# A list scheduler learns three more facts about the engines: the VectorE and GpSimd lock, measured durations, and the rate of a broadcast DMA

## The chip, the cores and the metric

The kernel runs on one core of one Trainium2 chip. The metric is the device time of one execution in microseconds (us), lower is better. A core has five instruction queues that run in order, each for itself: TensorE (PE, matmuls; its weight loads are listed as PEld), VectorE (DVE), ScalarE (ACT), GpSimd (POOL), and SyncE (SP), which issues the DMAs. Semaphores hold an instruction back until what it needs is there.

## The reference

The program is one block of a generator with two layers over 256 latent tokens and a prefix of 256 context tokens, 1024 features each, in float32. Cut to its frame:

```python
for layer in range(DEPTH):                       # DEPTH = 2
    mod_l, mod_c = ...                           # shift, scale, gate from silu(c) @ ada_w[layer]
    h = modulate(rmsnorm(x, g), shift, scale)    # latent and context tokens
    x = x + gate * (rglru_mixer(h) if layer == 0 else deltanet_mixer(h))
    h = modulate(rmsnorm(x, g2), shift2, scale2)
    x = x + gate2 * swiglu(h, w_gu, w_down)      # 1024 -> 2 x 2816 -> 1024
return rmsnorm(x, final_norm_g)                  # latent tokens
```

Layer 0 mixes tokens with a bidirectional gated linear recurrence (RG-LRU: input product, short convolution, gates, scan in both directions, output product). Layer 1 mixes them with a bidirectional gated DeltaNet: input product, short convolution and SiLU on q, k and v, then for each head and each chunk of tokens a unit triangular system is solved, and a state is carried over the chunks in both directions. Each layer ends in a SwiGLU feed-forward part.

## The kernel before

**Work.** Features lie on the 128 partitions, tokens along the free dimension. Every float32 product is made of three faster ones: a weight tile is loaded as `raw` [128, 1024], split into a high part `whi` and a remainder `wlo` (`weight()`, lines 636 to 646), and activations are split in the same way (`hh`, `hl`). `mm3()` issues whi with hh, whi with hl, wlo with hh into one PSUM bank. The copy that makes whi may go to ACT or DVE. The subtraction that makes wlo may go to DVE or POOL in layer 0, in both feed-forward parts and in the late DeltaNet work, and is fixed to POOL in most of the DeltaNet layer. There are three `raw` buffers and two each of `whi` and `wlo`.

**Stages.** 0 to about 240 us: modulation and the RG-LRU layer. 240 to 690: its output, the feed-forward part of layer 0, and the background sums of layer 1's modulation (`ada_steps`, tiles `x` and `ring`). 690 to 1275: the DeltaNet layer. 1275 to the end: the feed-forward part of layer 1. In the DeltaNet layer the program text runs stages in the order of the string `PROG`: A (input products; `conv_silu` evicts each product from PSUM by four operations that write `cu`, then SiLU), E (decays: a DMA spreads one row of the small DRAM array `rows` over all partitions into `gn`, eight affine_selects on POOL mask it, ACT takes exponentials), N (the triangular systems: `gn` is scaled, four 32-row transposes on DVE bring the diagonal blocks into `lw`, thirty pairs of `lmul` and `lw` operations on DVE solve them, two more transposes write `ld` and `ldt`), L (the off-diagonal blocks by small matmuls into `ps_w` and `ps_z`), P (attention weights: the same spread of `rows` into `qg`, affine_selects into `at`), C (the state: `ps_ks`, `ps_y`, `ps_s`, `ps_o`, with `kw`, `vb`, `S`, `oa`; a power on POOL gives `fo`, the norm of an output head; `nkh` is the like for a key head), Z and W (output gates and the output product). `scratch` holds the small tiles of the decay computation at the stage's start.

**Order.** Nothing is issued as written. Every instruction becomes an `_Op` of the `Recorder`, with its operands, its dependencies, a priority (its place in the text plus a bias per stage from `TUNE`), and for each engine that may run it a cost from `_cost()` (lines 257 to 296). At the end of a part of the program `flush()` (line 364 on) runs a list scheduler: it keeps a clock for each of the five engines, always takes the engine whose clock is least (PE, then DVE, ACT, POOL, SP at a tie), and gives it the ready instruction with the lowest priority number. `bank_free()` (line 475) says when the PSUM bank of an instruction is free of other engines; an instruction that would start over 40 ns later than its engine's clock is put back until then, and the engine takes another. An instruction with a choice is left to the other engine if that one would be done sooner. DMAs share one modelled channel of 360 bytes per ns with 2000 ns latency. Tiles take their buffers in program order. The order found is then emitted engine by engine, and the hardware queues run it strictly in that order, whatever the real durations are. So a cost does not change what an instruction takes; it changes the order of the queues and which engine gets an instruction.

Of the kernel before, what the change touches and what calls it, by code (L numbers as in the profile page):

```python
# [12 lines left out]
F32 = mybir.dt.float32  # L13
# [13 lines left out]
# columns of the packed small-parameter array  # L27
# [10 lines left out]
# ---------------------------------------------------------------- program order  # L38
# The kernel is written down stage by stage; a list scheduler then orders the instructions of all
# engines, earlier stages first, so that later independent work fills an engine's waits. Tiles are  # L40
# allocated when their first instruction is placed.
def _shuffle(sh, pattern, sizes):
    """einops-like rearrange of a numpy array"""
# [33 lines left out]
class _Tile:  # L77
    def __init__(self, pool, shape, dtype, tag, bufs, name, dram):
# [7 lines left out]
        # a bank of PSUM is one region: its readers wait for all products into it  # L86
# [6 lines left out]
        self.group = [-1] * 4       # last product into the bank, per 32 partitions  # L93
        self.used = {}              # a bank serves one engine at a time: its last use by each
# [5 lines left out]
class _AP:  # L100
    """an access pattern of a tile that may not have its place yet"""
# [34 lines left out]
    def raw(self, offset, ap):  # L136
        """any pattern over a DRAM tile"""
        return self._with(("raw", offset, ap), self.sh)
# [25 lines left out]
class _Op:  # L164
    __slots__ = ("alts", "args", "kw", "tiles", "deps", "prio", "idx", "bytes", "succ", "ndep", "ready", "fin", "rows", "cols", "narrow")


_TABLE = {"Tanh": 7, "Exp": 1, "Gelu_apprx_tanh": 2, "Silu": 4, "Sqrt": 8}     # sets that hold the function
# [28 lines left out]
class Recorder:  # L197
    DMA_RATE = 360.0        # bytes / ns
    DMA_LATENCY = 2000
    TICK, TICK_COLUMNS = 10240 / 3, 3300  # L200
    # from the end of an instruction to the start of one that waits for it
# [15 lines left out]
    # ---- instructions with a choice of engine  # L217
# [22 lines left out]
    def tt(self, out, a, b, op):  # L240
        """add, subtract or mult of SBUF operands"""
        self._any(("DVE", "tensor_tensor", (out, a, b, op), {}), ("POOL", "tensor_tensor", (out, a, b, op), {}))

    @staticmethod
    def mark(ap):
        """the instructions that have written ap so far, for after= of a later one"""
        return np.unique(ap.t.writer[ap.blocks()]).tolist()
# [8 lines left out]
    # ---- costs in ns  # L256
    def _cost(self, eng, method, out, ins, kw, args):
        n = out.free() if isinstance(out, _AP) else 1
        src_psum = any(i.t.psum for i in ins) or (isinstance(out, _AP) and out.t.psum)
        if eng == "PE":  # L260
# [8 lines left out]
            if m <= 64:         # the column groups run side by side  # L269
                first = out.sh.flat[0] < out.t.sh.size // 4  # L270
                return (max(4 * w / 2.4, 54) + 2) if first else 27 if m <= 32 else 54
            return max(4 * w / 2.4, 213) + 4
        if eng == "DVE":
            if method == "transpose":
                return 1.04 * n + 70
# [12 lines left out]
        if eng == "POOL":  # L288
            if method == "dma_start":
                return 1000  # L290
            if method in ("memset", "affine_select"):
                return 0.6 * n + 60
            if kw.get("op", args[3] if len(args) > 3 else None) == OP.pow:
                return 165 * n + 298
            return 2.2 * n + 100
        return 60

# [3 lines left out]
    def add_any(self, alts):  # L301
        """one instruction, on whichever of its engines is free first; alts hold the same operands"""
# [11 lines left out]
        op.alts = {}  # L314
        for eng, m, fn, a2, k2 in alts:
# [4 lines left out]
            op.alts[eng] = (self._cost(eng, m, out, ins, k2, a2), table, fn, a2, k2)  # L320
        op.bytes = 0
        if method == "dma_start":
            x = outs[0] if outs and not outs[0].t.dram else ins[0]
            op.bytes = 128 * 4 * x.free()
        eng = alts[0][0]
        op.rows = min(ins[0].sh.shape[0], 4) / 4 if eng == "PE" else 0      # share of the array's rows
        op.narrow = eng == "PE" and ins[0].free() <= 32
        op.cols = 0         # columns through the whole array
# [26 lines left out]
        if eng == "PE":     # accumulation groups of a bank stay in order  # L355
# [7 lines left out]
    # ---- order and emit  # L363
    def flush(self):
# [10 lines left out]
        # slots: the tiles of a tag take them in program order  # L375
# [27 lines left out]
        def offer(op):  # L403
            """all dependencies placed: a candidate once its tiles have slots"""
# [23 lines left out]
        dma_free, table, done = 0.0, 1, 0  # L428
        at_tick, columns, slow, rows, narrow = 0, 0.0, False, 1, False
        order = []  # L430
        while done < len(ops):
# [26 lines left out]
            if e == "PE" and op.rows != rows:  # L458
                # another tiling of the array costs a refill: stay with this one for a while
# [15 lines left out]
            def bank_free(op, e):  # L475
                return max((f + self.LATENCY[x][e] for t in op.tiles if t.psum for x, f in t.used.items() if x != e),
                           default=0.0)

            wait = bank_free(op, e)
            if len(op.alts) > 1:  # L480
                # leave it to another engine that would be done sooner
# [7 lines left out]
            if e == "PE":  # L489
                # the array runs at half its clock in a tick after one that kept it idle  # L490
# [23 lines left out]
            fin = clock[e]  # L514
            if op.bytes:
# [37 lines left out]
def hybrid_block(ctx: ExitStack, tc: tile.TileContext, I, out, dbg=None):  # L553
# [18 lines left out]
    def bank(tag, name="ps"):  # L572
        if tag == "mm" and cur["wide"]:     # the products take all banks but one in turn
# [11 lines left out]
    # ---------------------------------------------------------------- loads and constants  # L585
# [28 lines left out]
    # silu(c), silu(c_ctx) as the stationary operand of the modulation products  # L614
# [4 lines left out]
    sel4 = cp.tile([128, 2], F32, name="sel4")      # sums over the column groups of both streams  # L619
# [8 lines left out]
    # ---------------------------------------------------------------- weight streaming  # L628
# [7 lines left out]
    def weight(*src, cols=1024, aside=False, place=None):  # L636
        """hi + lo parts of a weight tile; aside: not on DVE"""
# [12 lines left out]
    def ahead(*srcs):  # L650
        """weights of the first products after this stage"""
# [11 lines left out]
    # ---------------------------------------------------------------- adaLN modulation  # L663
# [1056 lines left out]
```

## Time and profile before

| | |
|---|---|
| median of 3 runs | 1481.32 us (1480.1 to 1487.81) |
| span of the profiled execution | 1474.6 us; the page gives no time for what lies around it |
| instructions | 23548 |
| mean granted TensorE clock | 0.934 |
| ACT busy | 552.4 us (37%) |
| bytes moved by DMA | 208.26 MB, mean 141 GB/s |

How to read the lines of the profile: a row of the timeline gives start and length in us, engine, source line, operation, `out<-in` by tile names, shape, count, and in brackets how long the engine was idle before it and what ended that. All instructions carry line 544, where the order is emitted; they are told apart by tile names. A row of the waits gives the waiting engine and tile, what it waited for, total us, times and the longest. A row of the groups gives count, busy us, mean ns of one, and the idle time before the group. A row of the DMA list gives count, size and the median us from issue to landing.

### The profile page before, as it was taken

The page shows a single profiled execution, that of the slowest core. Times are in us where ns is not written, and L with a number is a line of the kernel's source. Part 1 is how long each engine was busy: PE and PEld are TensorE (multiplying, and loading weights), DVE is VectorE, ACT ScalarE, POOL GpSimd, SP SyncE. Part 2 cuts the span into 40 slices and gives each one's busy share as a digit, 9 for nine tenths or more (in the row PEclk, how much of TensorE's full clock was granted, in tenths as well). Part 3 has the DMA queues.
Part 4 walks back from the last instruction along what each step waited for, and adds up shares of the span by engine and source line. Part 5 has one row for each costly group of instructions (what it writes and reads, how often), then busy time and mean ns, then how long its engine had stood idle before and what let it go on. Part 6 is the DMA issues. An engine that isn't in the chain of part 4 may idle for free.

```text
span 1474.6 us, 23548 instructions
## 1 busy us (share of the span) xinstructions
PE 1329.7 (90%) x9195; PEld 1135.7 (77%) x9195; DVE 1149.3 (78%) x1802; ACT 552.4 (37%) x1069; POOL 430.8 (29%) x357
## 2 busy tenths in 40 slices
PE   6998989999999999988767997888888898899997
PEld 3676758787778777886656786777788797899997
DVE  6899996778888885577689578699698767777765
ACT  3365562342323231025666434735634531211100
POOL 2134341111122111122545332643543521122111
PEclk9999999999999999999978789699599899999999
DMA  9544433355544564333842115315235205455563
GB/s 355 193 146 142 155 115 104 139 190 190 177 171 172 173 206 120 105 123 122 190 132 90 50 56 131 95 65 151 88 100 136 95 12 181 139 186 180 177 186 116
DMA packets 69790, 208.26 MB, mean 141 GB/s; under 512 B 6960, under 2 KB 14384, under 8 KB 69424
## 3 DMA queue, kind: packets, MB, share of 16 engines
q1 hardware_dynamic: 69680, 206.77, 44.1%
q8 instruction: 72, 1.18, 0.3%
q14 instruction: 38, 0.31, 0.1%
HBM read 196.71 MB, written 10.03 MB: 140 GB/s over the span
## 4 chain that ended last, share of the span: by engine, by line
PE 28%; DVE 17%; issue 3%; DMA 3%; POOL 1%; ACT 1%; POOLq 0%; SPq 0%; DVEq 0%; ACTq 0%
PE ps_mm L544 13%; DVE lw L544 4%; PE ps_dn L544 4%; DVE cu L544 3%; DVE lmul L544 2%; DMA qg<-rows 2%; PE ps_z L544 2%; PE ps_wo L544 2%; PE ps_w L544 2%; PE ps_y L544 2%; DVE whi L544 1%; PE ps_o L544 1%; DVE gn L544 1%; PE ps_g L544 1%; PE ps_s L544 1%
## 5 line engine op out<-in xcount | busy, mean ns | idle before, releaser
L544 PE MATMUL ps_mm<-hh,whi 128*128 128x512 f32 (+1 forms) x888 | 340.6, 385 | 35.3 <-DVE cu L544 18.2
L544 PE MATMUL ps_mm<-hh,wlo 128*128 128x512 f32 (+1 forms) x888 | 337.6, 381 | 18.1 <-POOL wlo L544 12.3
L544 PE MATMUL ps_mm<-hl,whi 128*128 128x512 f32 (+1 forms) x888 | 337.4, 381 | 0.3 <-DVE hl L544 0.3
L544 POOL TENSOR_TENSOR wlo<-raw,whi 128x1024 fp32r<-128x1024 f32 (+1 forms) x69 | 171.9, 2493 | 379.4 <-DVE whi L544 141.9
L544 DVE CAST whi<-raw 128x1024 fp32r<-128x1024 f32 (+1 forms) x185 | 139.3, 753 | 136.9 <-PE ps_mm L544 68.2
L544 PEld LDWEIGHTS ps_mm<-hh,whi 128*128 128x128 f32 x888 | 178.6, 202 | 73.6 <-issue 26.7
L544 DVE TENSOR_TENSOR wlo<-raw,whi 128x1024 fp32r<-128x1024 f32 (+1 forms) x169 | 214.7, 1271 | 11.3 <-ACT whi L544 1.4
L544 PEld LDWEIGHTS ps_mm<-hh,wlo 128*128 128x128 f32 x888 | 178.6, 201 | 50.0 <-POOL wlo L544 14.9
L544 PEld LDWEIGHTS ps_mm<-hl,whi 128*128 128x128 f32 x888 | 178.7, 201 | 29.0 <-issue 1.6
L544 PE MATMUL ps_dn<-fh,wlo 128*128 128x256 f32 (+1 forms) x374 | 122.5, 328 | 0.9 <-DVE wlo L544 0.9
L544 PE MATMUL ps_dn<-fh,whi 128*128 128x256 f32 (+1 forms) x374 | 122.9, 329 | 0.3 <-DVE whi L544 0.3
L544 PE MATMUL ps_dn<-fl,whi 128*128 128x256 f32 (+1 forms) x374 | 122.3, 327 | 0.0
L544 PE MATMUL ps_mm<-h2h,whi 128*128 128x256 f32 x352 | 100.1, 285 | 1.2 <-ACT h2h L544 1.2
L544 PE MATMUL ps_mm<-h2l,whi 128*128 128x256 f32 x352 | 100.5, 286 | 0.2
L544 PE MATMUL ps_mm<-h2h,wlo 128*128 128x256 f32 x352 | 100.1, 285 | 0.1
L544 POOL TENSOR_TENSOR x<-x,ring 128x1024 f32<-128x1024 f32 x13 | 37.0, 2850 | 166.3 <-ACT ring L544 166.3
L544 ACT ACTIVATE whi<-raw 128x1024 fp32r<-128x1024 f32 (+2 forms) x53 | 54.7, 1033 | 79.6 <-PE ps_mm L544 32.9
L544 ACT ACTIVATE fh<-sg 128x256 fp32r<-128x256 f32 (+1 forms) x43 | 22.4, 522 | 157.7 <-DVE sg L544 157.7
L544 PEld LDWEIGHTS ps_dn<-fh,wlo 128*128 128x128 f32 x374 | 71.1, 190 | 7.7 <-DVE wlo L544 1.8
L544 PEld LDWEIGHTS ps_dn<-fh,whi 128*128 128x128 f32 x374 | 71.1, 190 | 7.5 <-DVE whi L544 0.7
L544 ACT ACTIVATE ring<-ring,cs 128x1024 f32<-128x1024 f32 x42 | 48.3, 1150 | 74.3 <-DVE x L544 74.2
L544 PEld LDWEIGHTS ps_dn<-fl,whi 128*128 128x128 f32 x374 | 71.1, 190 | 5.9
(309 smaller groups left out, 2868.0 us busy)
## 6 DMA issues: line engine op xcount, KB each, us to landing
ring<-ada_w SPq DMA_DIRECT2D x96, 512.0 KB, 4.7
raw<-ffn_gu SPq DMA_DIRECT2D x88, 512.0 KB, 3.6
raw<-dn_w_in SPq DMA_DIRECT2D x49, 512.0 KB, 3.5
raw<-ffn_down SPq DMA_DIRECT2D x34, 512.0 KB, 3.6
raw<-rg_w_in SPq DMA_DIRECT2D x16, 512.0 KB, 3.8
gn<-rows SPq DMA_DIRECT2D x4, 2048.0 KB, 15.5
raw<-ffn_down SPq DMA_DIRECT2D x17, 384.0 KB, 3.4
raw<-dn_w_out SPq DMA_DIRECT2D x12, 512.0 KB, 3.5
```

The source lines that it names most:

```text
L544: call(*[real(x) for x in args], **{n: real(v) for n, v in kw.items()})
```

## The change

Only the model inside the scheduler changes; stage order, biases, buffers and arithmetic stay as they are.

1. *Durations.* The DVE transpose costs 1.85 ns per column in place of 1.04; on POOL affine_select and memset get prices of their own, and other operations go from 2.2 n + 100 to 2.25 n + 30 ns.
2. *Lock.* Each instruction gets a class per engine from `_lock()`. On DVE class 1 is an operation with two wide SBUF inputs, class 2 a `tensor_copy` or `tensor_scalar` from SBUF to SBUF, 0 the rest, such as all that read only one tensor from SBUF beside PSUM. On POOL memset is class 2, all else but DMAs class 1. `flush()` keeps in `held` the end and class of the last operation of the other engine, and `bank_free()` also waits for that end where both classes are set and either DVE's is 2 or POOL's is 1.
3. *Broadcast.* A DMA from a pattern made by `.raw()` (the loads of `gn` and `qg` from `rows`) counts 2.3 times its bytes.

```diff
         if eng == "DVE":
             if method == "transpose":
-                return 1.04 * n + 70
+                return 1.85 * n + 70
...
-            if method in ("memset", "affine_select"):
-                return 0.6 * n + 60
+            if method == "affine_select":
+                return 1.1 * n + 30
+            if method == "memset":
+                return 0.87 * n + 25
             if kw.get("op", args[3] if len(args) > 3 else None) == OP.pow:
                 return 165 * n + 298
-            return 2.2 * n + 100
+            return 2.25 * n + 30
         return 60
+
+    @staticmethod
+    def _lock(eng, method, outs, ins):
+        if eng == "DVE":
+            wide = [x for x in ins if not x.t.psum and x.free() > 1]
+            if len(wide) > 1 or (len(wide) == 1 and method == "tensor_tensor" and len([x for x in ins if not x.t.psum]) > 1):
+                return 1
+            if method in ("tensor_copy", "tensor_scalar") and len(wide) == 1 and not outs[0].t.psum:
+                return 2
+            if method == "tensor_tensor" and len(ins) == 1 and wide:
+                return 1
+            return 0
+        if eng == "POOL":
+            return 2 if method == "memset" else 1 if method != "dma_start" else 0
+        return 0
...
+            op.lock[eng] = self._lock(eng, m, outs, ins)
...
             op.bytes = 128 * 4 * x.free()
+            if any(o[0] == "raw" for y in ins for o in y.ops):
+                op.bytes *= 2.3
...
             def bank_free(op, e):
-                return max((f + self.LATENCY[x][e] for t in op.tiles if t.psum for x, f in t.used.items() if x != e),
+                free = max((f + self.LATENCY[x][e] for t in op.tiles if t.psum for x, f in t.used.items() if x != e),
                            default=0.0)
+                mine, (until, theirs) = op.lock[e], held.get(e, (0.0, 0))
+                if mine and theirs:
+                    dve, pool = (mine, theirs) if e == "DVE" else (theirs, mine)
+                    if dve == 2 or pool == 1:
+                        free = max(free, until)
+                return free
...
             clock[e] += cost
             fin = clock[e]
+            if e in ("DVE", "POOL"):
+                held["POOL" if e == "DVE" else "DVE"] = (clock[e], op.lock[e])
```

More of the change, by code (lines that the diff above doesn't have):

```diff
@@ L164 @@
 class _Op:
-    __slots__ = ("alts", "args", "kw", "tiles", "deps", "prio", "idx", "bytes", "succ", "ndep", "ready", "fin", "rows", "cols", "narrow")
+    __slots__ = ("alts", "args", "kw", "tiles", "deps", "prio", "idx", "bytes", "succ", "ndep", "ready", "fin", "rows", "cols", "narrow",
+                 "lock")
 _TABLE = {"Tanh": 7, "Exp": 1, "Gelu_apprx_tanh": 2, "Silu": 4, "Sqrt": 8}
@@ L313, in add_any @@
         op.args, op.kw = a, k
-        op.alts = {}
+        op.alts, op.lock = {}, {}
         for eng, m, fn, a2, k2 in alts:
@@ L427, in flush @@
                 offer(op)
-        dma_free, table, done = 0.0, 1, 0
+        dma_free, table, done, held = 0.0, 1, 0, {}
         at_tick, columns, slow, rows, narrow = 0, 0.0, False, 1, False
```

## The prediction

> **What bounds the kernel now.** I read the head of the page first, then the busy times of the first three of four stages, then the list of who TensorE (PE) waits for, and last the instructions around the longest of its waits.
>
> ```profile
> span 1474.6 us, 23548 instructions
> PE 1329.7 (90%) x9195; PEld 1135.7 (77%) x9195; DVE 1149.3 (78%) x1802; ACT 552.4 (37%) x1069; POOL 430.8 (29%) x357
> 0.00:240.00 240.00, 215.43 (x1075) 152.13 (x1076) 205.01 (x316) 121.34 (x181) 68.27 (x58) 0.98 0.51 179
> 240.00:690.00 450.00, 435.75 (x2225) 356.29 (x2223) 347.26 (x415) 133.89 (x195) 84.32 (x41) 0.99 0.46 156
> 690.00:1275.00 585.00, 488.51 (x4326) 438.23 (x4325) 460.49 (x897) 275.70 (x640) 244.54 (x230) 0.85 0.37 106
> ```
>
> The columns of a stage are its length, then busy time of PE, weight loads, VectorE (DVE), ScalarE (ACT) and GpSimd (POOL), then the granted clock. In the first feed-forward stage (row two) PE is idle for 14.3 of 450 us: no order of the other engines can win much there, nor in the second one, which is built in the same way. The RG-LRU stage (row one) leaves 24.6 us idle, and the DeltaNet stage (row three) 96.5 us at a mean clock of 0.85. What the change can win lies there, in the waits of PE. The first six rows are of the DeltaNet stage, the last two of the RG-LRU stage:
>
> ```profile
> PE ps_mm L544 <- DVE cu L544: 18.2, 7, 6.2
> PE ps_mm L544 <- ACT whi L544: 8.7, 1, 8.7
> PE ps_mm L544 <- POOL wlo L544: 7.2, 4, 4.8
> PE ps_ot L544 <- DVE lmul L544: 4.6, 1, 4.6
> PE ps_mm L544 <- DVE lw L544: 4.6, 1, 4.6
> PE ps_mm L544 <- POOL wlo L544: 5.1, 3, 2.7
> PE ps_mm L544 <- POOL ol L544: 1.8, 1, 1.8
> ```
>
> **Part 1, the lock.** The planner now knows that DVE and POOL hold each other up. Is that so? At 798.8 us:
>
> ```profile
> 798.86 2.48 DVE L544 TENSOR_TENSOR lmul<-lw 128x168 f32<-128x168 f32 x1
> 801.27 0.73 DVE L544 SCALAR_TENSOR_TENSOR cu<-ps_mm,sm,cu 128x508 f32<-128x508 f32 x1
> 801.92 1.81 DVE L544 TENSOR_TENSOR lw<-lw,lmul 128x168 f32<-128x168 f32 x1
> 798.80 4.75 POOL L544 TENSOR_TENSOR wlo<-raw,whi 128x1024 fp32r<-128x1024 f32 x2 [2.79 <-DVE whi L544]
> 1015.41 0.32 DVE L544 TENSOR_TENSOR lmul<-lw 128x168 f32<-128x168 f32 x1
> 1015.76 0.33 DVE L544 TENSOR_TENSOR lw<-lw,lmul 128x168 f32<-128x168 f32 x1
> 1015.50 1.10 POOL L544 TENSOR_TENSOR nkh<-ssk,phalf 128x4 f32<-128x4 f32 x1 [7.41 <-DVE nbc L544]
> 687.08 0.29 DVE L544 SCALAR_TENSOR_TENSOR scratch<-scratch 128x128 f32<-128x128 f32 x1
> 688.54 2.75 DVE L544 SCALAR_TENSOR_TENSOR scratch<-scratch 128x128 f32<-128x128 f32 x2
> 691.87 2.00 DVE L544 SCALAR_TENSOR_TENSOR scratch<-scratch 128x128 f32<-128x128 f32 x1
> ```
>
> It is: lmul took 2.48 us and lw 1.81 beside two POOL wlo, and 0.32 and 0.33 elsewhere, while cu, which reads PSUM, kept its 0.73. Behind the two stood cu, the evictions that free the bank for PE: the longest of the seven cu waits. The lock cost (2.48 - 0.32) + (1.81 - 0.33) = 3.6 us of it. The scratch operations before another such wait lost (2.75 - 2 x 0.29) + (2.00 - 0.29) = 3.9 us. In the new plan DVE finds lmul blocked and takes cu first, which it classes as free. I take both: -7.5; bounds 0 (cu was not ready) and -18.2 (all seven). Late next at 799 is wlo itself, which ends at 803.55.
>
> In the RG-LRU stage PE waits 5.1 + 1.8 = 6.9 us for POOL. With the lock counted, an operation that may go to either engine looks dearer on POOL:
>
> ```profile
> L544 POOL TENSOR_TENSOR wlo<-raw,whi 128x1024 fp32r<-128x1024 f32 x13 | 36.8, 2832 | 67.6 <-ACT whi L544 24.8 <-PE ps_g L544 15.0 <-DVE whi L544 12.2
> L544 DVE TENSOR_TENSOR wlo<-raw,whi 128x1024 fp32r<-128x1024 f32 x15 | 18.3, 1222 | 0.8
> L544 DVE SCALAR_TENSOR_TENSOR iu<-iu,u 128x512 f32<-128x512 f32 x16 | 19.7, 1233 | 0.0
> 122.80 0.68 DVE L544 SCALAR_TENSOR_TENSOR iu<-iu,u 128x512 f32<-128x512 f32 x1
> ```
>
> Moving a wlo costs DVE 1.22 us and spares it a lock of up to 2.83; DVE is busy for 205 of 240 us, so it can't take all. Half of the wait: -3.5; bounds -6.9, and +7.1 if all thirteen move (13 x 1.22 = 15.9 us more on DVE) and only what iu lost to the lock (19.7 - 16 x 0.68 = 8.8 us) is won back.
>
> **Part 2, the broadcast's rate.** A DMA from the `rows` array now counts 2.3 times its bytes: 2.10 MB at 360 bytes/ns is 5.8 us plus 2, and becomes 13.4 plus 2.
>
> ```profile
> gn<-rows SPq DMA_DIRECT2D x4, 2048.0 KB, 15.5
> 717.14 0.69 DVE L544 CAST whi<-raw 128x1024 fp32r<-128x1024 f32 x1 [0.20 <-PE ps_mm L544]
> 719.22 5.67 POOL L544 TENSOR_SCALAR_AFFINE_SELECT gn<-gn 128x512 f32<-128x512 f32 x8 [4.44 <-DMA gn<-rows]
> 724.87 2.34 POOL L544 TENSOR_TENSOR wlo<-raw,whi 128x1024 fp32r<-128x1024 f32 x1
> 727.27 0.79 PE L544 MATMUL ps_mm<-hh,wlo 128*128 128x512 f32 x1 [4.82 <-POOL wlo L544]
> 1129.64 0.64 POOL L544 TENSOR_SCALAR_AFFINE_SELECT at<-qg 128x512 f32<-128x512 f32 x1 [10.10 <-DMA qg<-rows]
> 1130.25 1.01 POOL L544 TENSOR_TENSOR fo<-sso,nhalf 128x4 f32<-128x4 f32 x1
> 1132.55 1.09 PE L544 MATMUL ps_ot<-ident,oa 128*128 128x128 f32 x4 [4.62 <-DVE lmul L544]
> ```
>
> The chip took 15.5 us, so the new figure fits. The old one made POOL's queue wait: it stood idle 4.44 us for gn with a wlo behind the eight selects whose cast had ended at 717.83, and PE then waited 4.82 us for that wlo. At 1129.64 POOL had stood 10.10 us for qg with fo behind it, and PE waited 4.62 us for the transposes that need it. A planner that expects the broadcast later puts wlo and fo first: -9.4; bounds 0, and -11.8 if the rest of that stage's 7.2 us for POOL wlo goes with it. SP's queue gains nothing: the broadcasts keep their places, and a weight load behind one still lands late (PE's 8.7 us for ACT whi stays).
>
> **Part 3, the durations.** The affine_select and memset prices change little that anyone waits for; the transpose is the one that counts.
>
> ```profile
> L544 DVE STREAM_TRANSPOSE lw<-gn 32x1024 f32<-32x1024 f32 x16 | 31.6, 1978 | 0.2
> 728.29 0.63 PE L544 MATMUL ps_mm<-hl,whi 128*128 128x512 f32 x1
> 728.71 0.63 PE L544 MATMUL ps_mm<-hh,wlo 128*128 128x512 f32 x1
> 731.23 0.40 PE L544 MATMUL ps_mm<-hh,whi 128*128 128x512 f32 x1
> 731.47 0.39 PE L544 MATMUL ps_mm<-hl,whi 128*128 128x512 f32 x1
> ```
>
> It was planned at 1.04 x 1024 + 70 = 1135 ns, takes 1978, and is now planned at 1964. The DVE time is the same; only what stands between the transposes can move. In the 4.6 us wait on lw, cu stood behind three transposes, each 0.84 us longer than planned: -2.5; bounds 0 and -4.6. With the waits goes some slow clock: after the gap of 4.82 us PE's matmuls started 0.42 us apart instead of 0.24, and by 731.2 they were back. If the slow pace held from 727.3 to 731, those are nine matmuls x 0.18 us: 1.6 us. Four such gaps close in parts 1 and 2, 6.4 us; half, since the rows show it after one gap only: -3; bounds 0 and -6.4.
>
> **What it adds.** The choice of engine, the release of slots and all later orders follow the new clock, with the stage order and the biases unchanged. Two costs show in no row. The rule lets POOL start only when DVE's last locking operation is over, and at a tie DVE is taken first, so behind a run of such operations POOL is planned late; above, the chip let a wlo in between two of them. And a power on four columns counts as a lock for about 1 us, while nkh (1.10 us) ran beside lmul and lw of 0.32 and 0.33.
>
> By the Trainium skill (SBUF — State Buffer, "Who interferes with whom") a DVE instruction with two SBUF inputs contends with any GpSimd instruction that reads SBUF, and the first to issue blocks the other for the whole instruction. By that rule the charge for the powers is right, and the half of the next cost that I lay to it would go: 1466.5 in place of 1469. The nkh row speaks against it.
>
> ```profile
> L544 POOL TENSOR_TENSOR wlo<-raw,whi 128x1024 fp32r<-128x1024 f32 (+1 forms) x40 | 95.5, 2390 | 105.5 <-ACT whi L544 50.2 <-DVE whi L544 16.4 <-DVE lw L544 15.0
> ```
>
> PE's products need these forty, and behind each stand POOL's kw, vb and S and the next weight load, whose buffer it frees. If one wlo in each of the four lmul/lw runs comes a whole wlo late, that is 4 x 2.39 = 9.6 us; if none, 0: I take +4.8. Below 0 it can't lie: what DVE gains from a later POOL is in part 1. A new head of a queue somewhere is priced by the longest of PE's waits above, 8.7 us; with none, 0. I take one: +8.7.
>
> **The sum.** -7.5 - 3.5 - 9.4 - 2.5 - 3 + 4.8 + 8.7 = -12.4 us on the span of 1474.6. The median of the runs, 1481.32, stands 6.7 us above that span, which I keep: 1468.9, so 1469.
>
> **The rivals.** *Slower: POOL is planned late as a rule.* Place: the forty wlo of the DeltaNet stage. For it speaks that DVE is busy 460 of 585 us there, much of it in locking operations; against it, that POOL is busy only 245 and the chip grants it the lock in its turn. If every second one is a wlo late on PE's path, 20 x 2.39 = 48 us are lost against gains of 26: +22, 1503. It decides from about eleven late wlo on; a handful more than that gives 1489.
>
> *No change.* The planned waits close, but DVE bounds the stage (460 of 585 us): it is busy through the whole gap at 799, so PE's gaps move behind the next eviction. Then parts 1 and 3 give nothing, part 2 its 9.4, the costs stay at some 9 to 13: 1481 to 1485, at 1481.
>
> *All gains, no costs*: -26, 1455; POOL's 71% of free time speaks for it, the fixed biases against.
>
> **How the numbers follow.** Forecast 0.42, all gains 0.10, no change 0.21, slower 0.27. What a measurement can tell from no change is about 0.5%, 7.4 us; the forecast and the full gain lie beyond it: faster 0.52, same 0.21, slower 0.27. The range runs from 1448 (below the full gain, with part 1 nearer its bound) to 1497 (half of the slower cases); the likeliest case alone spans 1460 to 1474.
>
> **What would show it.** Part 1: DVE's wlo-side stretches shrink (lmul, iu and scratch nearer 0.3 to 0.7 us), and PE's wait for cu falls from 18.2 to about 10. Part 2: POOL's idle before gn and at falls, with wlo or fo ahead of them in its queue. Part 3: the wait on lw goes. Wrong it is if PE's wait for POOL wlo in the DeltaNet stage rises past 20 us, or if the stage's idle time stays at 96 us with other names in the list.

## The result: 1481 to 1430 us, and the profile after

The changed kernel takes 1429.7 us, the median of four runs (1424.51 to 1431.86), beside 1480.71 us for the kernel before in the same runs: a ratio of 0.965 with an interval of 0.9605 to 0.9694. The direction was forecast, the size was not: -51 us in place of -12.4. The profiled execution took 1428.36 us and has a span of 1426.6. Ratios, here and below, leave out executions more than 1.5% above the fastest of their kernel; among the kernels below this takes out two of wait_pool's four, and the profiled one of both_l0, which took 2109.43 us at a granted clock of 0.558.

Head of the page after:

```profile
span 1426.6 us, 23481 instructions
PE 1308.5 (92%) x9195; PEld 1126.8 (79%) x9195; DVE 1092.5 (77%) x1843; ACT 590.2 (41%) x1119; POOL 293.0 (21%) x273
```

PE has the same 9195 matmuls and is idle 118.1 us instead of 144.9; it is also busy 21.2 us less for the same work. GpSimd lost 84 of its 357 instructions and a third of its busy time, and VectorE, which took 41 more, is busy 57 us *less*.

To compare stages, both traces are cut, to within 0.6 us, at the same five places: the first output product of the RG-LRU layer, the first down product, the first key transposes of the DeltaNet layer, the first product of the last feed-forward part, and the end. First before, then after; columns as in the prediction, with DMA share and rate last.

```profile
0.00:208.80 208.80, 187.19 (x958) 130.38 (x959) 183.97 (x287) 113.08 (x167) 66.09 (x57) 0.98 0.54 190
208.80:525.90 317.10, 306.31 (x1507) 245.28 (x1505) 255.69 (x282) 99.06 (x135) 54.99 (x22) 1.00 0.47 162
525.90:680.70 154.80, 148.37 (x780) 124.68 (x781) 103.68 (x144) 35.77 (x57) 26.86 (x17) 0.98 0.41 130
680.70:1269.70 589.00, 493.21 (x4358) 442.13 (x4356) 464.14 (x901) 279.38 (x650) 249.19 (x232) 0.86 0.38 108
1269.70:1474.60 204.90, 194.64 (x1596) 193.24 (x1596) 141.84 (x191) 25.15 (x61) 33.70 (x29) 0.97 0.52 162
```

```profile
0.00:200.10 200.10, 182.15 (x959) 127.83 (x960) 164.42 (x293) 124.62 (x184) 18.59 (x38) 0.99 0.57 201
200.10:512.70 312.60, 306.37 (x1507) 248.75 (x1506) 229.98 (x273) 113.78 (x152) 41.21 (x18) 0.98 0.49 165
512.70:661.50 148.80, 145.46 (x780) 122.73 (x779) 95.28 (x137) 37.31 (x63) 24.54 (x16) 1.00 0.43 132
661.50:1220.60 559.10, 478.52 (x4358) 432.92 (x4356) 451.70 (x925) 288.04 (x659) 207.97 (x200) 0.87 0.39 114
1220.60:1426.60 206.00, 195.99 (x1596) 194.61 (x1596) 151.14 (x218) 26.44 (x62) 0.69 (x1) 0.96 0.51 162
```

Ahead of the DeltaNet layer -8.7, -4.5 and -6.0 us; in it -29.9; behind it +1.1. In the DeltaNet layer half of the gain is idle time of PE (95.8 to 80.6), half is PE needing 14.7 us less for its 4358 matmuls.

Rows that answer to those of the prediction. The RG-LRU stage (the window to 200 us for GpSimd, to 240 us for `iu`), and the row of the transposes in the DeltaNet layer:

```profile
L576 POOL TENSOR_TENSOR wlo<-raw,whi 128x1024 fp32r<-128x1024 f32 x3 | 7.4, 2481 | 21.9 <-PE ps_ada L576 15.0 <-ACT whi L576 6.2 <-DVE whi L576 0.8
L576 DVE SCALAR_TENSOR_TENSOR iu<-iu,u 128x512 f32<-128x512 f32 x16 | 11.0, 686 | 0.0
L576 DVE STREAM_TRANSPOSE lw<-gn 32x1024 f32<-32x1024 f32 x16 | 31.5, 1968 | 0.2
```

Three `wlo` are left on GpSimd there, and all sixteen `iu` take 0.69 us where the mean was 1.23. PE's longest waits in the DeltaNet layer after, and GpSimd's for the two broadcasts, which stood at 20.5 (`gn`) and 24.6 us (`qg`) before:

```profile
PE ps_w L576 <- DVE ldt L576: 13.6, 3, 8.0
PE ps_kq L576 <- DVE gn L576: 12.4, 2, 11.8
PE ps_mm L576 <- DVE cu L576: 7.8, 7, 3.1
PE ps_y L576 <- DVE lw L576: 7.4, 1, 7.4
PE ps_z L576 <- DVE lw L576: 4.7, 3, 3.7
POOL gn L576 <- DMA gn<-rows: 13.9, 3, 7.9
POOL at L576 <- DMA qg<-rows: 8.7, 3, 3.5
```

PE's wait for cu fell from 18.2 to 7.8 us; its wait for GpSimd's `wlo` fell from 7.2 to 0.4, and that of `ps_ot` for `lmul` (4.6) is gone. In their place stand the triangular systems: `ldt`, `gn` and `lw`. Here is the lock in the new order, at 760 us of the DeltaNet layer:

```profile
760.21 0.73 DVE L576 TENSOR_SCALAR cu<-ps_mm,sm 128x512 f32<-128x512 f32 x1
760.98 2.31 DVE L576 SCALAR_TENSOR_TENSOR cu<-ps_mm,sm,cu 128x508 f32<-128x508 f32 x3
763.21 0.47 DVE L576 TENSOR_SCALAR cu<-ps_mm,sm 128x256 f32<-128x256 f32 x1
763.72 1.52 DVE L576 SCALAR_TENSOR_TENSOR cu<-ps_mm,sm,cu 128x254 f32<-128x254 f32 x3
765.16 0.39 DVE L576 TENSOR_TENSOR lmul<-lw 128x234 f32<-128x234 f32 x1
766.02 0.41 DVE L576 TENSOR_TENSOR lmul<-lw 128x238 f32<-128x238 f32 x1
766.47 0.41 DVE L576 TENSOR_TENSOR lw<-lw,lmul 128x238 f32<-128x238 f32 x1
759.91 2.39 POOL L576 TENSOR_TENSOR wlo<-raw,whi 128x1024 fp32r<-128x1024 f32 x1 [0.81 <-ACT whi L576]
762.88 2.40 POOL L576 TENSOR_TENSOR wlo<-raw,whi 128x1024 fp32r<-128x1024 f32 x1 [0.58 <-ACT whi L576]
765.71 1.15 POOL L576 TENSOR_TENSOR nkh<-ssk,phalf 128x4 f32<-128x4 f32 x1 [0.43 <-DVE ssk L576]
```

While GpSimd makes two `wlo`, VectorE evicts two products (eight `cu`, none stretched), and the next `lmul` starts when the second `wlo` is over and takes 0.39 us. At 798.8 us of the kernel before, it stood in front of the evictions and took 2.48.

### The profile page after: what moved, and what is told of

It reads as the page before. It is cut to its first block, busy times and chain, and to the rows that moved or that the text cites. A ratio compares the mean times of both kernels' runs of the same rounds, so it can differ in the third digit from the quotient of the medians.

```text
span 1426.6 us, 23481 instructions
## 1 busy us (share of the span) xinstructions
PE 1308.5 (92%) x9195; PEld 1126.8 (79%) x9195; DVE 1092.5 (77%) x1843; ACT 590.2 (41%) x1119; POOL 293.0 (21%) x273
## 4 chain that ended last, share of the span: by engine, by line
PE 62%; issue 16%; DVE 11%; DMA 6%; ACT 3%; SPq 2%; POOL 0%; POOLq 0%; DVEq 0%; ACTq 0%
PE ps_mm L576 34%; PE ps_dn L576 9%; PE ps_g L576 4%; PE ps_ada L576 3%; PE ps_wo L576 2%; PE ps_z L576 2%; PE ps_o L576 2%; SPq L576 2%; PE ps_y L576 2%; DVE lw L576 2%; PE ps_w L576 2%; DVE cu L576 2%; DMA raw<-dn_w_in 1%; DMA spill<-on 1%; DMA kspill<-k 1%
## 5 line engine op out<-in xcount | busy, mean ns | idle before, releaser
L576 PE MATMUL ps_mm<-hh,whi 128*128 128x512 f32 (+1 forms) x888 | 330.8, 373 | 14.3 <-DVE cu L576 7.8
L576 PE MATMUL ps_mm<-hh,wlo 128*128 128x512 f32 (+1 forms) x888 | 327.1, 369 | 6.7 <-DVE wlo L576 4.6
L576 PE MATMUL ps_mm<-hl,whi 128*128 128x512 f32 (+1 forms) x888 | 326.2, 368 | 2.0 <-DVE hl L576 2.0
L576 DVE TENSOR_TENSOR wlo<-raw,whi 128x1024 fp32r<-128x1024 f32 (+2 forms) x189 | 233.3, 1234 | 26.4 <-ACT whi L576 18.3
L576 DVE CAST whi<-raw 128x1024 fp32r<-128x1024 f32 (+1 forms) x168 | 115.2, 686 | 143.6 <-PE ps_mm L576 69.2
L576 PEld LDWEIGHTS ps_mm<-hh,wlo 128*128 128x128 f32 x888 | 171.9, 194 | 36.1 <-DVE wlo L576 6.3
L576 PEld LDWEIGHTS ps_mm<-hl,whi 128*128 128x128 f32 x888 | 172.1, 194 | 26.6 <-DVE hl L576 2.2
L576 POOL TENSOR_TENSOR wlo<-raw,whi 128x1024 fp32r<-128x1024 f32 x49 | 118.7, 2423 | 234.5 <-ACT whi L576 101.4
L576 ACT ACTIVATE whi<-raw 128x1024 fp32r<-128x1024 f32 (+1 forms) x70 | 71.6, 1023 | 66.4 <-PE ps_mm L576 33.0
L576 POOL TENSOR_TENSOR x<-x,ring 128x1024 f32<-128x1024 f32 x13 | 34.3, 2635 | 212.6 <-ACT ring L576 212.6
L576 DVE SCALAR_TENSOR_TENSOR cu<-ps_mm,sm,cu 128x510 f32<-128x510 f32 (+2 forms) x96 | 64.9, 678 | 8.8 <-ACT cu L576 6.7
```

The source lines that it names most:

```text
L576: call(*[real(x) for x in args], **{n: real(v) for n, v in kw.items()})
```

## The experiments

Each ratio is to the kernel before as it ran on the same chip, where its median was 1480.54 to 1483.51 us. Durations of stages come from each kernel's trace, cut at the places named above, the DeltaNet layer at its first key transposes. A trace is one execution: the profiled one was 19 us quicker than the median of its kernel in wait_pool and 12 quicker in before_j3, 8 and 9 slower in no_dur and lock_choice, and within 7 us of it in the others. "cu" is PE's wait for `cu` in us, from the list of waits between 650 and 1290 us.

### Which part does it

The three parts are switched off singly and in pairs in the changed kernel:

```diff
-                if mine and theirs:          # no lock
+                if False:
-                op.bytes *= 2.3              # no broadcast rate
+                op.bytes *= 1
-                return 1.85 * n + 70         # no durations: transpose, and POOL's
+                return 1.04 * n + 70         # three prices, as before
```

One part alone:

> Before plus the lock alone (durations and broadcast rate as before). My theory: the lock is the main cause, by keeping two-way work off GpSimd where VectorE is busy (GpSimd gets 178 two-input operations instead of 257) and by ordering VectorE around what is left. It should win 35 of the 51 us: about 1445, with all 19 us ahead of the DeltaNet layer there (its start near 661, before 680.7). Rival 1 (broadcast and transpose prices make the gain of the DeltaNet layer): 1461, that is only the 19 us. Rival 2 (any new order scatters by 20 us or more, the cause is chance): anything from 1440 to 1500.

> Before plus the broadcast's rate alone. My theory: GpSimd's idle time ahead of its selects falls from 45 us to under 25 and about 9 us are won, all in the DeltaNet layer: 1472. Rival 1: 20 us or more, 1460 or less. Rival 2: anything from 1460 to 1500, with no tie to GpSimd's wait for the broadcast.

> Before plus the new durations alone (transposes, select, memset, GpSimd's other operations). My theory: 2 to 5 us, 1477, within what can't be told from no change. Rival 1: 10 us or more, 1470 or less. Rival 2: 1460 to 1500.

Two of the three:

> After without the lock (broadcast and durations stay). My theory: most of the gain is gone, 1468 to 1475, and the DeltaNet layer starts near 680 again. Rival 1: the DeltaNet layer keeps its 30 us, 1450. Rival 2: no relation to the other three runs.

> After without the broadcast's rate (lock and durations stay). The first four runs split the gain: all of the 19 us ahead of the DeltaNet layer come with the lock and go without it, while the DeltaNet layer took 560 us in after and 591 to 605 in the four. Theory I (interaction): in the DeltaNet layer the lock pays only in a model whose other prices are right; so this one, with one price wrong, lies between: that layer 575 to 590, in all 1445 to 1460, and the broadcast's price shows as a wait behind it. Theory C (chance): any new order of that layer falls somewhere between 560 and 605 whatever the model says; here about 598, 1467. The stages ahead of it: 661 by both.

> After without the new durations (lock and broadcast stay). Theory I: between lock alone and after again, DeltaNet layer 575 to 590, in all 1445 to 1460. Theory C: about 598 for the layer, 1467 in all, no tie to the transposes. The stages ahead of it: 661 by both.

| kernel | parts | median us | ratio to before, interval | DeltaNet layer begins | its length | cu |
|---|---|---|---|---|---|---|
| before | none | 1480.71 | | 680.3 | 590.0 | 18.2 |
| bcast_only | broadcast | 1478.41 | 0.9964 (0.9940 to 0.9989) | 683.5 | 591.1 | 25.2 |
| dur_only | durations | 1491.4 | 1.0033 (1.0008 to 1.0058) | 679.0 | 599.2 | 26.4 |
| no_lock | both of these | 1492.44 | 1.0048 (1.0023 to 1.0074) | 683.1 | 604.1 | 17.4 |
| lock_only | lock | 1469.25 | 0.9895 (0.9856 to 0.9935) | 658.1 | 604.7 | 1.9 |
| no_bcast | lock, durations | 1455.07 | 0.9822 (0.9802 to 0.9842) | 659.7 | 588.4 | 7.9 |
| no_dur | lock, broadcast | 1441.29 | 0.9734 (0.9704 to 0.9764) | 662.7 | 579.2 | 6.2 |
| after | all | 1429.7 | 0.9650 (0.9605 to 0.9694) | 661.1 | 560.1 | 7.8 |

Two columns split cleanly by the lock. With it the DeltaNet layer begins some 20 us earlier, whatever the other prices are; and with it PE's wait for cu is 2 to 8 us, without it 17 to 26. The length of the layer does not split so: with the lock alone it is 604.7 although cu is down to 1.9, and only with the other two prices does it come to 560. So the parts do not add: the broadcast's rate gains 0.4% by itself and 25 us on top of the other two (1455.07 to 1429.7), the durations lose 0.3% by themselves and gain 12 us on top (1441.29 to 1429.7). What was expected of the first four missed: lock_only came out 24 us above the 1445 that it was to give, bcast_only 6 us above its 1472, and dur_only and no_lock, which were to be faster than the kernel before, were 0.3 and 0.5% slower. Theory I, written after these four, has the layer's length right for the other two.

Where the layer's time goes with the lock but without the broadcast's rate is seen in the waits of no_bcast:

```profile
POOL at L576 <- DMA qg<-rows: 48.6, 5, 23.9
PE ps_mm L576 <- POOL wlo L576: 17.1, 4, 11.8
1019.80 1.23 POOL L576 TENSOR_SCALAR_AFFINE_SELECT at<-qg 128x512 f32<-128x512 f32 x2 [13.45 <-DMA qg<-rows]
1023.98 0.64 POOL L576 TENSOR_SCALAR_AFFINE_SELECT at<-qg 128x512 f32<-128x512 f32 x1 [2.95 <-DMA qg<-rows]
1024.59 2.34 POOL L576 TENSOR_TENSOR wlo<-raw,whi 128x1024 fp32r<-128x1024 f32 x1
1026.98 0.58 PE L576 MATMUL ps_mm<-hh,wlo 128*128 128x256 f32 x1 [11.83 <-POOL wlo L576]
```

GpSimd stands 13.45 and then 2.95 us for broadcasts that the plan expects too early, with a `wlo` behind them, and PE waits 11.83 us for that `wlo`; all its waits of this kind come to 17.1 us, and to 7.2 in the kernel before. (The longest wait for a broadcast, 23.9 us, has no `wlo` right behind it.) With the lock alone other heads of queues stand there:

```profile
PE ps_w L574 <- DVE ldt L574: 18.8, 4, 16.1
PE ps_mm L574 <- ACT whi L574: 14.0, 3, 13.3
PE ps_ot L574 <- DVE oa L574: 12.1, 1, 12.1
```

### Is it the luck of an order

Any new price gives a new order, so a meaningless one was tried: the modelled latency from VectorE to PE, 256 ns, shifted by 20 ns either way, in the kernel after and in the one before.

```diff
-                   "DVE": {"PE": 256, ...
+                   "DVE": {"PE": 236, ...      # _j3; 276 in _j4
```

> After with one latency of the model, from VectorE to TensorE, 20 ns shorter (236 in place of 256 ns): a change without meaning that sets many choices anew, in the same model otherwise. Theory I: the model is what pays, so the DeltaNet layer stays at 555 to 572 and the time at 1422 to 1442. Theory C: the layer scatters like the others, 575 to 605, 1445 to 1475.

> After with the same latency 20 ns longer (276 ns). Theory I: DeltaNet layer 555 to 572, 1422 to 1442 us. Theory C: 575 to 605, 1445 to 1475. By both the stages ahead of that layer stay near 661, since the lock's gain there does not hang on one order.

> Before with the model's latency from VectorE to TensorE 20 ns shorter, the same meaningless edit as in after_j3: how far does chance alone move the old model's plan? Theory I (the model pays, not one lucky order): the DeltaNet layer stays within 580 to 605, not near 560, the stages ahead of it near 680; 1470 to 1495 in all. Theory C (chance): one of this and the next reaches 570 or less in that layer.

> Before with the same latency 20 ns longer. Theory I: DeltaNet layer 580 to 605, 1470 to 1495 in all. Theory C: 570 or less in this or in the last one.

Measured: after_j3 1434.52 us, after_j4 1433.65; before_j3 1480.77, before_j4 1491.15 (ratios 0.9677, 0.9664, 0.9989 and 1.0060). The gain is no single lucky order. The DeltaNet layer took 579.5 and 607.6 us in the two traces of the kernel before, against 590.0, and 567.9 and 563.4 in those of the kernel after, against 560.1. Not all of that is the order's doing: the 579.5 is from the quickest of ten executions of before_j3, 1469.1 to 1485.66 us, whose median is that of the kernel before. Between single traces of single orders, a difference of some 10 us in that layer is therefore not evidence, and neither are the +14.7 us of lock_only there nor the small losses of dur_only and no_lock. The medians of whole executions part more clearly: those with all three prices in which VectorE waits for the lock lie between 1418.96 and 1434.52 us (both_l0, below, lower still), no_dur at 1441.29, and all others at 1455.07 or more. In the total, the broadcast's 20 to 25 us on top of the others (1455.07 against 1429.7 to 1434.52) stand clear of the scatter; the durations' 7 to 12 do not surely.

### Which use of the lock

Two theories were to be told apart. By the one, that of the prediction, VectorE takes unlocked work, cu above all, while GpSimd holds the lock (V); by the other, GpSimd gives way to VectorE and is left with less of the shared work (Y). `bank_free()` is asked twice: to make an instruction wait in the plan, and to compare two engines that could take it. In lock_choice only the comparison (for both engines) knows the lock, in lock_wait only the wait; cut to the line that says it:

```diff
-            wait = bank_free(op, e)                       # lock_choice
+            wait = bank_free(op, e, False)                # False: without the lock
...
-                other = min((max(clock[x], bt, bank_free(op, x)) ...          # lock_wait
+                other = min((max(clock[x], bt, bank_free(op, x, False)) ...
```

> After with the lock counted only where an instruction with a choice of engine is given away, not where an instruction waits for the lock. 200 two-input operations stay on GpSimd (after 165 to 175, before 257). Theory K (the choice is what pays: less work on GpSimd): the stages ahead of the DeltaNet layer near 661 to 668, and most of the gain stays, 1435 to 1450. Theory W (the waiting pays: VectorE takes unlocked work while GpSimd holds the lock): near no_lock, 1470 to 1490.

> After with the lock counted only where an instruction waits, not in the comparison of engines. 169 two-input operations on GpSimd, as few as in after, since what waits for the lock on GpSimd is picked up by VectorE meanwhile. Theory K: close to after because GpSimd's share is as small, 1430 to 1445. Theory W: close to after as well. The two part in lock_choice; here both fall if it is over 1455.

Then the wait was given to one engine alone (`if e == "DVE" and mine and theirs` in wait_dve, "POOL" in wait_pool), and a kernel without the lock kept every `tt()` with a choice off GpSimd (dve_only), to see whether less work there is all that the lock brings:

> After with only VectorE waiting for the lock; GpSimd ignores it in the plan. 299 two-input operations on GpSimd, more than the 257 of before. Theory Y: no gain or a loss, 1485 to 1510, with VectorE's stretched time at 130 us or more (before 159, after 69). Theory V: a good part of the gain stays, 1440 to 1460.

> After with only GpSimd waiting for the lock; VectorE ignores it in the plan. 179 two-input operations on GpSimd (after 173). Theory Y (GpSimd's yielding pays: its work moves to VectorE or behind VectorE's runs): the stages ahead of the DeltaNet layer at 661, that layer 560 to 572, 1428 to 1442 in all. Theory V (VectorE's filling with unlocked work pays, as the prediction reckoned): 1460 to 1485.

> After without the lock in the model, and every subtraction, sum or product that may go to either engine fixed to VectorE: 61 two-input operations stay on GpSimd, those fixed to it. Theory S (it is enough to keep such work off GpSimd): the stages ahead of the DeltaNet layer at 655 to 665 and that layer at 575 or less, 1425 to 1445. Theory T (the timing of what stays on GpSimd matters too): the 19 us ahead are won, but the DeltaNet layer, where GpSimd keeps its fixed work, stays at 585 to 605; 1450 to 1475.

| kernel | median us | ratio, interval | RG-LRU | to first down product | to DeltaNet | DeltaNet | cu | two-input operations on GpSimd |
|---|---|---|---|---|---|---|---|---|
| before | 1480.71 | | 208.8 | 317.1 | 154.4 | 590.0 | 18.2 | 257 |
| lock_choice | 1473.35 | 0.9935 (0.9908 to 0.9963) | 203.2 | 313.2 | 152.8 | 607.1 | 17.2 | 200 |
| dve_only | 1474.52 | 0.9962 (0.9930 to 0.9995) | 194.2 | 307.9 | 153.0 | 608.3 | 18.6 | 61 |
| wait_pool | 1461.81 | 0.9778 (0.9672 to 0.9885) | 197.8 | 314.1 | 154.9 | 569.6 | 13.6 | 179 |
| wait_dve | 1431.0 | 0.9643 (0.9589 to 0.9697) | 208.1 | 309.0 | 149.6 | 557.4 | 2.1 | 299 |
| lock_wait | 1430.22 | 0.9658 (0.9627 to 0.9690) | 199.3 | 309.4 | 149.8 | 568.9 | 5.9 | 169 |
| after | 1429.7 | 0.9650 (0.9605 to 0.9694) | 200.1 | 312.7 | 148.4 | 560.1 | 7.8 | 173 |

The wait carries the gain; the comparison alone is worth 0.65%. Of the wait, VectorE's side does it: wait_dve has all of the gain with *more* work on GpSimd than before, so theory Y falls for the total. It had something for it in dve_only's first stages, but the DeltaNet layer of that kernel is as long as any, and theory S falls with it. Its row of busy times and two rows of its trace (the layer's window, and PE's wait for cu):

```profile
PE 1316.0 (90%) x9195; PEld 1134.8 (77%) x9195; DVE 1143.9 (78%) x1959; ACT 567.4 (39%) x1106; POOL 166.4 (11%) x161
655.10:1263.40 608.30, 490.12 (x4360) 441.14 (x4360) 487.83 (x999) 289.66 (x675) 136.85 (x112) 0.85 0.35 105
PE ps_mm L576 <- DVE cu L576: 18.6, 7, 5.3
```

And the same three of wait_dve:

```profile
PE 1313.0 (92%) x9195; PEld 1134.9 (79%) x9195; DVE 1072.9 (75%) x1705; ACT 600.3 (42%) x1132; POOL 470.8 (33%) x399
666.70:1224.10 557.40, 483.38 (x4359) 439.97 (x4359) 437.63 (x871) 291.49 (x671) 260.62 (x248) 0.86 0.38 114
PE ps_mm L576 <- DVE cu L576: 2.1, 3, 1.3
```

GpSimd is busy 261 us of the layer in the one and 137 in the other, and it is the one with 261 that is 51 us shorter: what counts there is theory V, that VectorE takes evictions and other unlocked work while GpSimd holds the lock. The timelines show it directly. Summed over the DeltaNet layer, GpSimd's operations (memsets left out) ran beside a `cu` of VectorE for 25 to 35 us in each of the nine traces in which VectorE does not wait for the lock (34.0 before, 34.3 in wait_pool, 25.1 in dve_only), and for 48 to 55 us in each of the ten in which it does (50.0 after, 54.9 in wait_dve). wait_pool stays half open. Its four times lie between 1442.58 and 1466.69, its ratio is that of the two quicker ones, and its stages are those of the quickest; cu, at 13.6, is between the two groups.

In the RG-LRU stage it is the other way round: wait_dve has nothing of the gain (208.1) with 16 `wlo` on GpSimd to 200 us, and the kernels with few there have it: 3 in the kernel after, 1 in dve_only, at 194.2 the shortest stage of this table; lock_choice, with 8, lies between. The two gains have different causes.

### The powers, and both causes together

pow_free takes the charge for the small powers out of the lock. both_l0 does that too and moves every `tt()` ahead of the DeltaNet layer to VectorE; dve_l0 does the latter on wait_dve.

```diff
+            if any(i.free() <= 4 for i in outs):     # _lock(), POOL: pow_free, both_l0
+                return 0
+        if self.vec:                                 # tt(): both_l0, dve_l0
+            return self.V.tensor_tensor(out, a, b, op)
-    cur["wide"] = False
+    cur["wide"], R.vec = False, False                # where the DeltaNet layer begins
```

> After with GpSimd operations of up to four columns (the powers, two border memsets) put in no lock class, as the trace of before showed for nkh beside lmul. The prediction laid about half of 4.8 us to this false charge: 1424 to 1428 if it was right. If it does not matter: 1427 to 1436.

> pow_free, and everything up to the DeltaNet layer that may go to VectorE or GpSimd fixed to VectorE. If the two causes are separate: RG-LRU stage 194 to 197 in place of 201.7, down to the DeltaNet layer about 651 in place of 663, that layer 559 as it was (its plan does not change), 1413 to 1420 in all. If they hang together, the DeltaNet layer changes by more than 5 us, or the total stays at 1426.

> wait_dve (only VectorE waits for the lock), and layer 0 fixed to VectorE likewise. Separate causes: RG-LRU stage 194 to 197 in place of 208.1, the layer's feed-forward part as in wait_dve or 2 us better, the DeltaNet layer 557, 1412 to 1420 in all. If GpSimd's yielding is what the RG-LRU stage needs, and not the lesser work, it stays at 205 or more.

pow_free takes 1426.2 us, ratio 0.9603 (0.9535 to 0.9671): too near to the kernel after to be told from it. both_l0 takes 1409.74, 1412.57 and 1417.5, ratio 0.9549 (0.9495 to 0.9603); of it only these times are used. dve_l0 takes 1418.96, ratio 0.9581 (0.9534 to 0.9629). Each has a median 12 to 14 us below that of the kernel that it adds the move to (1422.17 to 1429.16 and 1429.88 to 1431.54); by the ratios, which allow for the chip, it is 8 to 9 us. Both are below every other kernel here. The stages of dve_l0, against wait_dve: RG-LRU 198.1 (208.1), then 306.4 (309.0), 149.5 (149.6) and DeltaNet 561.3 (557.4). So the move does its work in the RG-LRU stage, by 10.0 us, though the stage stayed longer than expected; the two causes nearly add.

## Where the prediction was wrong, and where it was right

**By stage.** Forecast against measured, in us of the span: the RG-LRU stage -3.5 and -8.7, the feed-forward part of layer 0 nothing and -10.5, the DeltaNet layer -8.9 and -29.9 (in idle time of PE -5.9 and -15.2, in its pace -3 and -14.7), the last feed-forward part nothing and +1.1: -12.4 and -48.0. The medians are 3 us further apart, since what lies between span and median, kept at 6.7 us, became 3.1. The mechanism was largely the right one; the steps that failed are the price of the slow clock, the stage that was put at nothing, the RG-LRU term and the costing of one wait at a time. (In the prediction's list of waits, five rows are of the DeltaNet stage and two of the RG-LRU stage.)

**Part 3, the slow clock: the term that was mis-sized most.** It said -3, with -6.4 as the most, from four gaps that close. In the DeltaNet layer PE was busy 14.7 us less for the same matmuls. The clock records of the traces account for most of that. Summed over the stretches of the layer in which the granted clock was half, first before, then after:

```profile
sum 167.80, PE 134.63; mean PE 7.48
sum 140.60, PE 103.77; mean PE 9.43
```

There are 18 such stretches before and 11 after. PE was busy 31 us less at half the clock. By the prediction's rows matmuls start 0.42 us apart at the slow pace and 0.24 at the full one, so an estimated 13 of the 14.7 us are the clock's. The pace was thus lost in far more places than the four gaps that were priced. Its size is that of one execution each: PE's busy time at half clock is 104 to 131 us in the seven traces with all three prices in which VectorE waits for the lock, and 123 to 154 in the eight in which neither engine does.

**Part 1, DeltaNet: right in kind, short by a little.** VectorE does take cu first where it finds `lmul` blocked. PE's wait for cu fell by 10.4 us where -7.5 was taken. That the lock does this is shown: ten kernels in which VectorE waits for the lock in the plan have it at 1.9 to 9.7 us, the eight in which neither engine waits for it at 17.2 to 26.4. That it is not enough for the layer, lock_only showed.

**Part 1, RG-LRU: mis-sized, and past its bound.** It said -3.5, half of the 6.9 us that PE waits for POOL there, and the stage became 8.7 us shorter. The step that failed was to take PE's *named* waits for GpSimd as the most to be won, and to count as won back on VectorE only what one form (`iu`, 8.8 us) lost. Summed over all forms, each against what the same form takes undisturbed (its 15th percentile), VectorE lost 39 us in the first 240 us, and 9 after. Over all traces the stage follows that loss: 194.2 to 202.2 us long where VectorE loses 6 to 12, 203.2 to 205.6 where it loses 27 to 34, 207.4 to 208.8 where it loses 39 to 50. So moving ten `wlo` did not cost VectorE 1.22 us each: its busy time in the stage fell from 184.0 to 164.4. The upper bound of +7.1 rested on the same step. Of the 8.7 us, 3.7 are idle time of PE and 5.0 its pace; wait by wait, how VectorE's time reaches PE is not shown.

**The feed-forward part of layer 0 was written off.** "No order of the other engines can win much there", since PE was idle for only 14.3 of 450 us. Between 208.8 and 680.7 us it won 10.5: 7.6 of its 17.2 us of idle time, and 2.9 of busy time. wait_dve, which wins nothing in the RG-LRU stage, has this gain (309.0 and 149.6).

**Part 2: the waits did as said, the price did not.** GpSimd's idle time before `gn` and `at` fell from 45.1 to 22.6 us. In the full change the two waits that the term was made of went as well, `wlo` from 7.2 to 0.4 us and `lmul` from 4.6 to nothing. But GpSimd's idle time fell further in bcast_only, to 12.3 us (6.8 and 5.5), and PE's two waits fell there to 2.6 and 2.3, yet the kernel gained 0.4% and not 9.4 us: PE waited 25.2 us for cu there (18.2 before) and 13.6 of `ps_kq` for `gn` (2.1). The new price fits `gn` alone. The loads of `qg`, 512 KB each, took 19.6 us in the median and at least 9.8 before, where 512 KB at 360 bytes per ns, times 2.3, plus 2 makes 5.4; how much of that is a wait behind other transfers is not shown.

**Part 3, the transposes.** PE's 4.6 us wait of `ps_mm` on `lw` went, and 7.4 us of `ps_y` on `lw` came. Alone the durations gave no gain.

**The costs.** The forty late `wlo` did not come (+4.8): the wait of `ps_mm` for them in the layer fell from 7.2 to 0.4. New heads of queues did (+8.7): `ldt` went from 4.9 to 13.6 and `ps_kq` on `gn` from 2.1 to 12.4, more than one.

**The sum.** What failed most is that it was a sum. Each term was read from one wait of the old order and taken as worth the same with and without the others. The experiments show the broadcast's rate worth 0.4%, or 25 us where the lock is in the model. The likely reason, argued and not shown, is that an order is only as good as its worst wrong price, for the engine that is planned wrong carries its error into the queues of the rest; no_bcast, with its 17.1 us for `wlo`, is the one place where that was seen directly. In the DeltaNet layer PE's waits that became shorter fell by 56 us in all, and those that became longer grew by 40. The prediction's rows are only part of the falls: they leave out `ps_y` on `r` (9.0 to 2.1), waits of `ps_w` and `ps_z` whose cause the profile doesn't show (14.0 to 6.1) and a dozen small ones, and ACT's `whi`, which was to stay, fell from 8.7 to 3.5. Three quarters of the rises are in the triangular systems (`ldt`, `gn`, `ps_y` and `ps_z` on `lw`, 31 us together). Which price brought which wait stays open.

**The rivals.** "Planned late as a rule" did not happen: PE's wait for `wlo` in the layer all but went. "No change" fell too, since PE's gaps did not merely move: its idle time in the layer fell by 15.2 us. "All gains, no costs" at 1455 was the nearest; the kernel came out 25 us below it and 18 below the low end of the range. For the powers, the trace after has the row again: `nkh` ran for 1.15 us beside `lmul` and `lw` of 0.41. As far as the trace's spans of GpSimd go, this speaks against the Trainium skill (SBUF — State Buffer, "Who interferes with whom"), by which a GpSimd instruction that reads SBUF holds up any VectorE instruction with two SBUF inputs. With the same section's other rule, that a VectorE instruction with at most one SBUF input is free outside the 2-port performance modes, the trace agrees, if the narrow `sm` is not counted: cu, with one wide SBUF tensor beside PSUM, kept its 0.73 to 0.77 us beside `wlo`.

## What to carry to other kernels

Where two engines share a lock, sum what each form of instruction loses against its own undisturbed time, since the lists of waits don't show it: VectorE lost 159 us so in the kernel before, 153 of them in instructions beside which one of GpSimd ran, and 69 after. That sum is no price either (dve_only lost 67 and gained 0.4%, wait_dve lost 121 and gained 3.6%): a planner that fills such times with work that does not need the lock gains more than one that moves the work away, unless, as in the RG-LRU stage, the work costs the other engine less than the lock did; try both. And prices in a planner are not to be costed one by one: switch them off in pairs, and shift a meaningless one to learn what the order alone scatters, over several executions of each.

## What the hardware showed that had not been expected

The lock costs GpSimd too: a `wlo` of the same shape took 2.83 us in the crowded RG-LRU stage before and 2.48 after. One that began at 125.15 us, while `th`, a VectorE operation with two SBUF inputs, had 0.47 us to go, took 2.72; with nothing of that kind beside it, it takes 2.34. And executions of one kernel scatter though all of them run the same queues: before_j3's ten by 16.6 us, and the four of the kernel after from 1424.51 us at a mean granted clock of 0.945 to 1431.86 at 0.930.
